# A hybrid decoder block on one core: norms and memory attention planned together with the causal attention, token tiles first

## The chip, the cores and the metric

The kernel runs on one core of one Trainium2 chip. The metric is the device time of one execution in microseconds; the time before is a median of 3 runs, 1797.26 us (1796.97 to 1797.59).

## The reference, cut to what matters

A decoder block over 1024 tokens of width 1024, with 256 memory tokens. Three gated branches run in parallel on the normed tokens, and a squared-ReLU MLP follows.

```python
h = rmsnorm(x, g_mix_norm)                         # x: 1024 x 1024
proj = h @ w_in                                    # sb q,k,v | fox q,k,v | forget | mem q | gates
o_sb  = stick_breaking_attention(sb_q, sb_k, sb_v)            # 8 heads of 64, causal
o_fox = forgetting_attention(norm(fx_q), norm(fx_k), fx_v, log_f)   # 8 heads of 64, causal
mh = rmsnorm(mem, g_mem_norm)                      # mem: 256 x 1024
mk, mv = split(mh @ w_mem_kv)                      # 4 heads of 128
o_mem = softmax(norm(mq) @ norm(mk).T / sqrt(128)) @ mv
x = x + (sum of gate_b * (o_b @ w_branch_b)) @ w_out
x = x + relu(rmsnorm(x) @ w_ff_up)**2 @ w_ff_down
```

Every product is taken in float32 accuracy by splitting each operand into a high part (a rounded copy, made on ScalarE) and a low part (the rest, made on VectorE), and by three matmuls: high by high, high by low, low by high.

## The kernel before, in words

**Names.** PE, DVE, ACT, POOL and SP are TensorE, VectorE, ScalarE, GpSimd and SyncE. `hTh` and `hTl` (tiles `hi`, `lo` in the trace) hold the normed tokens, transposed, high and low. `whi`, `wlo` are the split weights, `raw` the weights as loaded, `xt` a tile of 128 tokens by 1024, `st` a small tile of statistics with 1 to 16 columns, `gb` the norm's gain spread over 128 partitions, `xg` a tile times its gain, `xs` half a normed tile. Buffers of memory banks: `pp` for dense products, `sc` for scores, `tr` for transposes, `pv` for attention outputs.

**First part, written out by hand (lines 649 to 877).** The order of the code is the order of issue, which the compiler's tile scheduler may loosen a little. `normed_T` (L165) norms one tile: on ACT a square with a running sum (L163), on DVE the inverse root in 11 small steps (`rsqrt`, L124 to 137: a seed in two steps, and three rounds of three), a scaling, on PE eight 128x128 transposes (L186), on ACT the high part (L189) and on DVE the low part (L190). The two memory tiles are normed first, with the gain and the scaling in one DVE step (L181) that reads the spread gain from a bank. The eight token tiles follow, two ahead of each of the four memory key and value projections (`norm_x`, L678); their gain is multiplied in on POOL, as two halves of 128x512 (L172), and the scaling is a DVE step (L179). `halves` and `load_w` load and split the weights, `natural` takes the products (`mm3`, L157 to 159). Then come the queries of the memory attention (`mem_queries`), the memory attention itself (`mem_attention`, L753 to 791) and the first pair of stick-breaking heads' queries and keys.

**Second part, a planner (from L876).** At build time a small event simulation, the `Machine`, decides the order of the instructions. Processes are Python generators that yield an `Op` (an engine, an estimated cost, a function that emits instructions), `Get` a buffer, `Sleep`, or wait for an `Event`. An engine that is free in the simulation takes the ready operation with the lowest due time, and what it takes is emitted; each engine on the chip then runs its stream in that order. Attention units, dense projections (`Task`: gates, values, queries, keys), the weight loader and the first two branch products are such processes. Dense operations are marked `side`, and `PACE` says after how much dense work each attention unit may begin. A dense operation is a piece of at most 6 matmuls of 512 columns (`PIECE`) or 12 of 256. The forgetting attention scales its softmax rows on DVE (L1143).

**Third part (from 945 us on in the profile):** the third branch, the output projection and the MLP, ordered by hand.

## Time and profile before

| | before |
|---|---|
| median of 3 runs | 1797.26 us |
| the profiled execution, time | 1799.35 us |
| its span | 1797.6 us |
| PE busy | 1758.4 us (98%) |
| DVE busy | 1287.7 us (72%) |
| ACT busy | 801.7 us (45%) |
| POOL busy | 160.4 us (9%) |

The profiled execution lies 2.1 us above the median of the runs, and its span is 1.75 us shorter than its own time. A row of the timeline reads: start, duration, engine, line, operation, output<-inputs, partitions x elements, and in brackets how long the engine had been idle and what ended it. Matmuls are pipelined: the duration of one includes its latency, so the rate of a stream is read from the distance of two starts. A row of the windows reads: the stretch, its length, then busy time and count of instructions of PE, PEld (its weight loads), DVE, ACT and POOL, then the granted TensorE clock, the DMA share and GB/s.

### The profile page before, as it was taken

The numbers are of one execution on the slowest core, as the hardware profiler recorded it, in microseconds if no ns is written. First come the engines' busy times: TensorE is split into PE (matmuls) and PEld (weight loads), VectorE is DVE, ScalarE is ACT, GpSimd is POOL, SyncE is SP. The second block draws the span as 40 slices with busy tenths as digits, with TensorE's granted clock in tenths as the row PEclk, the third lists the DMA queues.
The fourth block names the chain that finished last, engine by engine and source line by source line (L and its number), as shares of the span: only waits on it lengthen the run. The fifth ranks groups of instructions, "written<-read, shape, count | busy, mean of one in ns | idle before, by whom it ended". The sixth has DMA issues, their size and how long they took to land.

```text
span 1797.6 us, 26005 instructions
## 1 busy us (share of the span) xinstructions
PE 1758.4 (98%) x9800; PEld 1517.0 (84%) x9800; DVE 1287.7 (72%) x2221; ACT 801.7 (45%) x1466; POOL 160.4 (9%) x283
## 2 busy tenths in 40 slices
PE   8899999999999999999999999899999999999999
PEld 6797998889888899899888899787888888788887
DVE  7986666656756577777998752587777775878786
ACT  5355545545555466556754332433323334333332
POOL 2200101111111100000000012011121120000000
PEclk9998999999999999999999999999999999999999
DMA  6211111231231311212344552224444464545433
GB/s 201 70 54 47 30 39 48 68 94 31 68 95 57 89 52 43 71 52 75 119 149 139 164 191 82 95 88 141 146 147 157 139 213 153 178 169 170 157 117 135
DMA packets 137441, 194.67 MB, mean 108 GB/s; under 512 B 9826, under 2 KB 81506, under 8 KB 137316
## 3 DMA queue, kind: packets, MB, share of 16 engines
q1 hardware_dynamic: 128836, 165.22, 28.9%
q0 software_dynamic: 8480, 27.79, 4.4%
q8 instruction: 77, 1.26, 0.3%
q14 instruction: 48, 0.39, 0.1%
HBM read 137.67 MB, written 55.31 MB: 107 GB/s over the span
## 4 chain that ended last, share of the span: by engine, by line
PE 86%; DVE 9%; ACT 2%; issue 2%; DMA 1%; SPq 0%; POOL 0%; ACTq 0%; DVEq 0%; POOLq 0%
PE pp L1326 33%; PE pp L231 9%; PE pp L619 5%; PE sc L231 5%; PE pv L1198 4%; PE tr L1178 4%; PE pp L159 3%; PE pp L157 3%; PE pp L158 3%; PE sc L619 3%; PE tr L619 3%; PE tr L231 2%; PE pv L619 2%; PE sc L157 2%; PE sc L158 1%
## 5 line engine op out<-in xcount | busy, mean ns | idle before, releaser
L1326 PE MATMUL pp<-hi,whi 128*128 128x512 f32 x480 | 192.8, 402 | 0.0
L1326 PE MATMUL pp<-lo,whi 128*128 128x512 f32 x480 | 189.1, 394 | 0.0
L1326 PE MATMUL pp<-hi,wlo 128*128 128x512 f32 x480 | 188.9, 394 | 0.0
L231 PE MATMUL pp<-h,oh 128*128 128x512 f32 x512 | 160.2, 394 | 2.7 <-ACT cu L398 2.7
L1326 PE MATMUL pp<-whi,hi 128*128 128x256 f32 (+1 forms) x512 | 145.6, 284 | 0.0
L1326 PE MATMUL pp<-whi,lo 128*128 128x256 f32 (+1 forms) x512 | 143.9, 281 | 0.0
L1326 PE MATMUL pp<-wlo,hi 128*128 128x256 f32 (+1 forms) x512 | 143.8, 281 | 0.0
L1185 DVE TENSOR_TENSOR ptl<-tr,pth 128x512 fp32r<-128x512 f32 (+1 forms) x160 | 100.0, 633 | 45.3 <-ACT pth L1183 44.5
L1183 ACT ACTIVATE pth<-tr 128x512 fp32r<-128x512 f32 (+1 forms) x160 | 87.1, 557 | 94.2 <-PE tr L1178 53.1
L619 PE MATMUL pp<-h,sop 128*128 128x512 f32 x504 | 118.6, 392 | 0.0
L231 PEld LDWEIGHTS pp<-h,oh 128*128 128x128 f32 x512 | 96.0, 188 | 25.0 <-ACT cu L398 3.5
L619 PEld LDWEIGHTS pp<-h,sop 128*128 128x128 f32 x504 | 94.5, 188 | 21.5 <-DVE sop L252 0.9
L1326 PEld LDWEIGHTS pp<-hi,wlo 128*128 128x128 f32 x480 | 90.2, 188 | 21.4
L1326 PEld LDWEIGHTS pp<-hi,whi 128*128 128x128 f32 x480 | 90.4, 188 | 16.2
L1326 PEld LDWEIGHTS pp<-lo,whi 128*128 128x128 f32 x480 | 90.5, 189 | 15.8
L231 PE MATMUL pp<-h,ol 128*128 128x512 f32 x256 | 101.0, 395 | 0.0
L1094 DVE TENSOR_TENSOR_SCAN r<-r,sm 128x896 f32<-128x896 f32 (+3 forms) x64 | 87.6, 1369 | 14.5 <-POOL r L1089 14.3
L1326 PEld LDWEIGHTS pp<-wlo,hi 128*128 128x128 f32 x512 | 96.5, 188 | 0.4
L1326 PEld LDWEIGHTS pp<-whi,hi 128*128 128x128 f32 x512 | 96.4, 188 | 0.4
L1326 PEld LDWEIGHTS pp<-whi,lo 128*128 128x128 f32 x512 | 96.5, 189 | 0.0
L1251 DVE TENSOR_TENSOR wlo<-raw,whi 128x1024 fp32r<-128x1024 f32 (+1 forms) x58 | 70.6, 1219 | 31.2 <-ACT whi L1250 30.7
L1198 PE MATMUL pv<-pth,v 128*128 128x256 f32 x320 | 85.4, 289 | 0.0
(373 smaller groups left out, 4590.3 us busy)
## 6 DMA issues: line engine op xcount, KB each, us to landing
raw<-w_in SPq DMA_DIRECT2D x42, 512.0 KB
raw<-w_up SPq DMA_DIRECT2D x64, 256.0 KB
s_scr<-s POOLq DMA_DIRECT2D x56, 256.0 KB, 2.7
ur<-s_scr SPq DMA_DIRECT2D x14, 1024.0 KB
gate_scr<-o SPq DMA_DIRECT2D x48, 256.0 KB
s_scr<-cu POOLq DMA_DIRECT2D x42, 256.0 KB, 2.9
ur<-s_scr SPq DMA_DIRECT2D x14, 768.0 KB
o<-gate_scr SPq DMA_DIRECT2D x32, 256.0 KB
```

Source lines behind the costliest of these rows:

```text
L157: nc.tensor.matmul(ps, lh, rh, start=(i == 0), stop=False)
L158: nc.tensor.matmul(ps, lh, rl, start=False, stop=False)
L159: nc.tensor.matmul(ps, ll, rh, start=False, stop=(i == n - 1))
L231: nc.tensor.matmul(ps, w[a_][:, k * P:(k + 1) * P], h[b_][k], start=(first and k == 0 and i == 0), stop=(last and k == 3 and i == 2), skip ...
L619: nc.tensor.matmul(ps, a_[:, c, q], b_[:, c, :], start=(kind in ("P1", "P2", "P7") and c == 0 and i == 0), stop=(kind in ("P2", "P4", "P3" ...
L1094: nc.vector.tensor_tensor_scan(out=rev, data0=rev, data1=zero.to_broadcast([P, n]), initial=1.0, op0=ALU.mult, op1=ALU.add)
L1178: nc.tensor.transpose(tr[:, jj * 256 + a * P:jj * 256 + (a + 1) * P], es[a][:, j * P:(j + 1) * P], ident)
L1183: yield Op("ACT", act_time(512 - lo_c), lambda: nc.scalar.activation(ph[:, lo_c:], tr[:, lo_c:], AF.Copy))
L1185: yield Op("DVE", dve_time(512 - lo_c), lambda: nc.vector.tensor_tensor(pl[:, lo_c:], tr[:, lo_c:], f32(ph[:, lo_c:]), ALU.subtract))
L1198: nc.tensor.matmul(pv[0][:, c_:256], v_of[key][:, j, h4, :], p_[:, jj * 256 + c_:(jj + 1) * 256], start=(k == 0 and n_ == 0 and i == 0), s ...
L1251: yield Op("DVE", dve_time(m), lambda: nc.vector.tensor_tensor(lo, raw, f32(hi), ALU.subtract))
L1326: nc.tensor.matmul(ps, a_, b_, start=(first and i == 0), stop=(last and i == n - 1))
```

## The change

1. The planner moves ahead of the first part, and the whole first part becomes its processes. `prologue` starts the token tiles in groups, [x0], [x1], [x2, x3], [x4, x5], [x6, x7], and then the memory tiles [m0, m1]; `norm` takes one inverse root per group, so there are six of 11 steps where there were ten. Every tile but the first gets its gain on POOL, in place and whole (128x1024), and one DVE scaling of 128x1024. `xt` has 7 buffers.
2. Both gains are spread to `gb` by four matmuls of one row at the very start (`spread`).
3. The first dense task is the values of the first stick-breaking heads, which need only token tiles and start as these come; the four memory projections (`dense_kv`), the first pair's queries and keys and the memory queries (`dense_mq`) follow as dense tasks, and the memory attention is a planned process whose scores and products mingle with dense work. The causal units wait for the memory keys, values and queries.
4. A dense operation is a piece of three matmuls of 512 columns, or six of 256.
5. The scaling of the forgetting attention's softmax goes from DVE to ACT. The copies of the memory keys and queries out of their banks go from DVE to ACT as well (`head_squares`).
6. The planner's model of a load becomes a shared pipe (250 bytes per ns and 2.0 us), `PACE` goes from 80 to 66 for the first four pairs, and `Machine.choose` lets an operation that needs another ACT table wait up to 4 us for others with the loaded one.

```diff
-    def load_time(size):
-        return 2.3 + size / 180e3
+    def transfer(fn, size, issue=0.1):
+        yield Op("SP", issue, fn, 0.0)
+        machine.pipe = max(machine.now, machine.pipe) + size / 250e3
+        yield Sleep(machine.pipe + 2.0 - machine.now)
...
+    N = Pool("n0", gb=2, xt=7, xj=1)
...
-    PIECE = mm_time(512) * 6
+    PIECE = mm_time(512) * 3
...
+    def norm(keys, late):
...
+        def gain(xt):
+            yield spread_
+            yield Op("POOL", 2.6, lambda: nc.gpsimd.tensor_tensor(xt, xt, gb, ALU.mult))
+        for i, key in enumerate(keys):
...
+            yield Op("ACT", 1.25, lambda: nc.scalar.activation(junk, xt, AF.Square, accum_out=ss[:, i:i + 1]))
+            if by_pool:
+                gained.append(spawn(gain(xt)))
+        r = yield from rsqrt_ops(ss, n, 1.0 / D)
+        for i, key in enumerate(keys):
+            xt, ri, s = x_in[key][0], r[:, i:i + 1], key[1]
+            if by_pool:
+                yield gained[i]
+                yield Op("DVE", 0.67, lambda: nc.vector.tensor_scalar(xt, xt, ri, None, ALU.mult))
...
+                evs.append(spawn(norm_half(key, xt, k4), late))
...
+        keys = [[("x", 0)], [("x", 1)], [("x", 2), ("x", 3)], [("x", 4), ("x", 5)], [("x", 6), ("x", 7)],
+                [("m", 0), ("m", 1)]]
+        spawn(fetch_tokens([k for ks_ in keys for k in ks_]))
+        evs = [spawn(norm(ks_, 3.0 * i), 3.0 * i) for i, ks_ in enumerate(keys)]
...
-            nc.vector.tensor_scalar(e[:, :n], e[:, :n], rl, None, ALU.mult)
...
+        yield Op("ACT", act_time(n), lambda: nc.scalar.activation(e[:, :n], e[:, :n], AF.Copy, scale=rl))
...
-                for k in range(0, KD, 2):
-                    ab = [x_ for kk in (k, k + 1) for x_ in passes(tuple(t[:, kk, :] for t in w),
-                                                                   (hTh[:, kk, cs], hTl[:, kk, cs]))]
+                for k in range(KD):
+                    ab = passes(tuple(t[:, k, :] for t in w), (hTh[:, k, cs], hTl[:, k, cs]))
...
+    h_tasks += [kv_tasks[0], sb_projection(0, True), kv_tasks[1], sb_projection(0, False), *kv_tasks[2:], dense_mq(0), dense_mq(1)]
...
-    PACE = [80.0 * min(c, 4) + 60.0 * max(c - 4, 0) for c in range(9)]
+    PACE = [66 * min(c, 4) + 60 * max(c - 4, 0) for c in range(9)]
```

The counts of matmuls are the same. The order changes from the start to the middle; the last 3854 PE instructions, from inside the second branch on, and the last 733 of DVE stand in the same order in both kernels.

POOL at the start of the program, in the order of issue. In the kernel before, each token tile `xt` gives two halves of a separate tile `xg`:

```order
L172 TENSOR_TENSOR xg_220<-xt_215,gb_191 128x512 x2
L172 TENSOR_TENSOR xg_265<-xt_260,gb_191 128x512 x2
L172 TENSOR_TENSOR xg_404<-xt_399,gb_191 128x512 x2
L172 TENSOR_TENSOR xg_449<-xt_444,gb_191 128x512 x2
L172 TENSOR_TENSOR xg_588<-xt_583,gb_191 128x512 x2
L172 TENSOR_TENSOR xg_633<-xt_628,gb_191 128x512 x2
L172 TENSOR_TENSOR xg_741<-xt_736,gb_191 128x512 x2
L172 TENSOR_TENSOR xg_786<-xt_781,gb_191 128x512 x2
```

POOL at the same place after the change. `xt_126` to `xt_131` are the token tiles x1 to x6, `xt_125` is x7, and the last two rows, with the gain `gb_141`, are the memory tiles m0 and m1:

```order
L869 TENSOR_TENSOR xt_126<-xt_126,gb_140 128x1024
L869 TENSOR_TENSOR xt_127<-xt_127,gb_140 128x1024
L869 TENSOR_TENSOR xt_128<-xt_128,gb_140 128x1024
L869 TENSOR_TENSOR xt_129<-xt_129,gb_140 128x1024
L869 TENSOR_TENSOR xt_130<-xt_130,gb_140 128x1024
L869 TENSOR_TENSOR xt_131<-xt_131,gb_140 128x1024
L869 TENSOR_TENSOR xt_125<-xt_125,gb_140 128x1024
L869 TENSOR_TENSOR xt_126<-xt_126,gb_141 128x1024
L869 TENSOR_TENSOR xt_127<-xt_127,gb_141 128x1024
```

Eight tiles in sixteen steps became nine tiles in nine steps, since the memory tiles now go this way too and only x0 does not.

DVE in the middle of the start-up, before: the end of an inverse root (L133 to 136) with the low part of a weight and of a memory tile in between, then the two scalings of the first token tile:

```order
L136 SCALAR_TENSOR_TENSOR st_235<-st_232,st_230 128x1
L133 SCALAR_TENSOR_TENSOR st_237<-st_235 128x1
L150 TENSOR_TENSOR wlo_390<-raw_387,whi_389 128x1024
L190 TENSOR_TENSOR v_99<-tr_184,v_99 128x4x128
L134 TENSOR_TENSOR st_237<-st_237,st_223 128x1
L136 SCALAR_TENSOR_TENSOR st_240<-st_237,st_235 128x1
L179 TENSOR_SCALAR xs_242<-xg_220,st_240 128x512
L179 TENSOR_SCALAR xs_244<-xg_220,st_240 128x512
```

DVE after, at the end of the start-up: the last rounds of the memory tiles' inverse root (L821 to 823, two columns at once), between them the scaling (L884) of x7 (`xt_125`) and then of m0 (`xt_126`), and the low parts (L915) of what PE has transposed:

```order
L821 SCALAR_TENSOR_TENSOR st_420<-st_421 128x2
L822 TENSOR_TENSOR st_420<-st_420,st_418 128x2
L823 SCALAR_TENSOR_TENSOR st_419<-st_420,st_421 128x2
L884 TENSOR_SCALAR xt_125<-xt_125,st_380 128x1024
L821 SCALAR_TENSOR_TENSOR st_420<-st_419 128x2
L822 TENSOR_TENSOR st_420<-st_420,st_418 128x2
L823 SCALAR_TENSOR_TENSOR st_421<-st_420,st_419 128x2
L884 TENSOR_SCALAR xt_126<-xt_126,st_421 128x1024
L915 TENSOR_TENSOR lo_98<-tr_109,hi_97 128x4x128
L915 TENSOR_TENSOR lo_98<-tr_110,hi_97 128x4x128
L1538 TENSOR_TENSOR v_123<-pp_106,v_123 128x8x64
```

The memory tiles, which opened DVE's work before, now close the start-up.

PE at its first rows, before: the spread of the memory gain, the transposes of the first memory tile, and the first products with it (`v_99` holds the normed memory):

```order
L200 MATMUL sc_107<-row_104 128x512
L200 MATMUL sc_109<-row_104 128x512
L186 MATMUL tr_137<-ident,xs_133 128x128 x4
L186 MATMUL tr_144<-ident,xs_135 128x128 x4
L157 MATMUL pp_307<-whi_205,v_99 128x256
L158 MATMUL pp_307<-wlo_206,v_99 128x256
L159 MATMUL pp_307<-whi_205,v_99 128x256
```

PE after, where the last normed tile (m1, `xt_127`) is transposed: ahead of it and behind it stand products with the values' weights (`whi`, `wlo`, L1466) and token tiles, and then the first products of 512 columns, with other weights (`whi_136`):

```order
L1466 MATMUL pp_104<-wlo_133,hi_97 128x256
L1466 MATMUL pp_104<-whi_132,lo_98 128x256
L906 MATMUL tr_109<-ident,xt_127 128x128 x4
L906 MATMUL tr_110<-ident,xt_127 128x128 x4
L1466 MATMUL pp_104<-whi_134,hi_97 128x256
L1466 MATMUL pp_104<-wlo_135,hi_97 128x256
L1466 MATMUL pp_104<-whi_134,lo_98 128x256
```

What PE does ahead of m1 is now only transposes and the values of the token tiles.

More of the change, by code (lines that the diff above doesn't have):

```diff
@@ new lines, in tile_hybrid_block, with spread @@
+    h_made, m_made = [Event() for _ in range(ST)], [Event() for _ in range(2)]
+    x_in, two_in = {}, Event()
+    gains = {k: (N.t("gb", [P, D]), Event()) for k in ("x", "m")}
+    junk = N.t("xj", [P, D])
+    ones_ = OB.free.popleft()
+    ones = ones_[:1, :P]
+    def spread(key, rows, landed):
+        gb, ev = gains[key]
+        yield landed
+        for half in range(2):
+            cs = slice(half * 512, half * 512 + 512)
+            sc = yield Get(SC)
+            yield Op("PE", 4 * mm_time(512), lambda: nc.tensor.matmul(
+                sc, ones, rows[half][:1], start=True, stop=True))
+            yield Op("ACT", act_time(512), lambda: nc.scalar.activation(gb[:, cs], sc, AF.Copy))
+            SC.put(sc)
+        machine.fire(ev)
@@ L1228, in units @@
     def units(large):
+        yield kv_over
+        for ev in mq_made.values():
+            yield ev
+        base = machine.side
         for c, pair in enumerate(pairs):
@@ L1445, in may @@
             n = 8 if keys else 4
-            if len(HT.free) < n:
+            if len(HT.free) < n or c and not all(ev.fired for ev in mq_made.values()) or not keys and sb_taken[0] < 2 * c + 1 \
+                    or keys and sb_taken[0] < 2 * c:
                 return False
+            sb_taken[0] += 1
             tiles_.extend(HT.free.popleft() for _ in range(n))
@@ L1800, in all_h @@
         machine.fire(closed)
[L1802 removed]
+    PACE = [66 * min(c, 4) + 60 * max(c - 4, 0) for c in range(9)]
     with tc.manual_schedule():
+        spawn(prologue())
+        for load in h_tasks[0].loads:
+            spawn(first_weights(load))
+        spawn(memory())
+        spawn(after_kv(kv_tasks))
         spawn(all_h([t.done for t in h_tasks]))
```

651 lines of the change are left out of this document (355 added, 296 removed).

## The prediction

> **What bounds the kernel now.** I first read the page's busy times and its slices, to see which engine is short and where.
>
> ```profile
> PE 1758.4 (98%) x9800; PEld 1517.0 (84%) x9800; DVE 1287.7 (72%) x2221; ACT 801.7 (45%) x1466; POOL 160.4 (9%) x283
> PE   8899999999999999999999999899999999999999
> DVE  7986666656756577777998752587777775878786
> PEclk9998999999999999999999999999999999999999
> ```
>
> PE is busy 98% of the span, and only three slices of 45 us fall below nine tenths: the first two and one near 900 us. In the second slice DVE stands at nine. Next I read the windows over the stretches that the change touches.
>
> ```profile
> core 0: us, PE busy (x) PEld busy (x) DVE busy (x) ACT busy (x) POOL busy (x), PEclk, DMA share, GB/s
> 0.00:45.00 45.00, 36.16 (x221) 30.69 (x222) 35.14 (x98) 24.48 (x36) 11.07 (x14) 0.96 0.65 201
> 45.00:90.00 45.00, 36.03 (x272) 34.06 (x271) 41.78 (x119) 16.29 (x28) 12.57 (x10) 0.92 0.24 69
> 90.00:135.00 45.00, 44.56 (x335) 41.79 (x334) 37.14 (x89) 23.27 (x59) 0.00 (x0) 1.00 0.18 54
> 135.00:180.00 45.00, 40.72 (x194) 32.67 (x193) 29.64 (x71) 24.23 (x61) 0.00 (x0) 0.89 0.15 47
> 180.00:800.00 620.00, 619.36 (x3864) 552.52 (x3862) 412.33 (x712) 327.56 (x667) 61.92 (x129) 1.00 0.21 59
> 800.00:945.00 145.00, 142.53 (x854) 124.74 (x854) 125.06 (x308) 91.84 (x195) 0.00 (x0) 0.99 0.37 114
> 945.00:1798.00 853.00, 839.07 (x4074) 700.48 (x4072) 606.64 (x827) 293.99 (x426) 74.80 (x130) 1.00 0.43 147
> ```
>
> From 180 to 800 us PE idles 0.64 us, and from 800 to 945 us 2.47 us. The rest of the program has one order in both kernels. So what can be won lies in the first 180 us. There PE idles 22.5 us by these rows, but the loss is larger, since a busy matmul at half clock hides some. I count the work instead, by the forms that PE runs there and the distance of two starts.
>
> ```profile
> L157 PE MATMUL pp<-whi,hi 128*128 128x256 f32 x128 | 37.0, 291 | 0.3 <-ACT hi L189 0.3
> L186 PE MATMUL tr<-ident,xs 128*128 128x128 f32 x80 | 12.8, 306 | 4.7 <-DVE xs L179 3.3 <-DVE xs L181 1.4
> L158 PE MATMUL pp<-lo,whi 128*128 128x512 f32 x32 | 12.8, 399 | 0.0
> L200 PE MATMUL sc<-row 1*128 1x512 f32 x8 | 6.1, 882 | 5.9 <-DVE st L129 5.9
> ```
> ```profile
> 17.54 0.28 PE L158 MATMUL pp<-wlo,v 128*128 128x256 f32 x1
> 17.66 0.28 PE L159 MATMUL pp<-whi,v 128*128 128x256 f32 x1
> ```
> ```profile
> 78.71 1.07 PE L186 MATMUL tr<-ident,xs 128*128 128x128 f32 x8 [0.20 <-DVE xs L179]
> ```
> ```profile
> 873.05 0.40 PE L1326 MATMUL pp<-lo,whi 128*128 128x512 f32 x1
> 873.28 0.39 PE L1326 MATMUL pp<-hi,wlo 128*128 128x512 f32 x1
> ```
>
> With all lines of a form together, the first 180 us hold 681 matmuls of 256 columns, 140 of 512, and 184 transposes. Warm, one of 256 starts 0.12 us after the last, one of 512 0.23 us; eight transposes take 1.07 us with about 0.28 us of latency at the end, so 0.11 us each. The work is 681 x 0.12 + 140 x 0.23 + 184 x 0.11 + 6.1 for the spread gains = 140.2 us. **PE loses 39.8 us of the first 180.** This is the pot.
>
> **The change, part by part.**
>
> *The start-up.* After the change PE's order up to m1's transposes holds 180 products of 256 columns, 72 transposes and the spread: 180 x 0.12 + 72 x 0.11 + 6.1 = 35.6 us. If PE gets past m1 at the time T, it has lost T - 35.6 by then. T is set by DVE, which norms every tile; I add up DVE's rows in the new order up to m1's scaling.
>
> ```profile
> 0.81 0.86 SPq L666 DMA_DIRECT2D xt<-mem  x2
> 1.72 0.33 SPq L196 DMA_DIRECT2D row<-g_memn  x1
> ```
> ```profile
> 4.33 1.06 ACT L163 ACTIVATE xg<-xt 128x1024 f32<-128x1024 f32 x1 [2.23 <-DMA xt<-mem]
> 5.29 0.19 ACT L163 ACTIVATION_READ_ACCUMULATOR xg<-xt 128x1 f32 x1
> ```
> ```profile
> 5.89 0.16 DVE L133 SCALAR_TENSOR_TENSOR st<-st 128x1 f32<-128x1 f32 x1
> 6.09 0.16 DVE L134 TENSOR_TENSOR st<-st,st 128x1 f32<-128x1 f32 x1
> ```
> ```profile
> L150 DVE TENSOR_TENSOR wlo<-raw,whi 128x1024 fp32r<-128x1024 f32 x14 | 18.2, 1300 | 1.5 <-ACT whi L149 1.3
> L190 DVE TENSOR_TENSOR lo<-tr,hi 128x512 fp32r<-128x512 f32 x16 | 10.4, 683 | 0.3 <-ACT hi L189 0.2
> L181 DVE SCALAR_TENSOR_TENSOR xs<-xt,st,sc 128x512 f32<-128x512 f32 x4 | 2.9, 746 | 0.0
> ```
> ```profile
> L1143 DVE TENSOR_SCALAR e<-e,st 128x1024 f32<-128x1024 f32 x8 | 6.0, 754 | 0.3
> ```
>
> The first tile's square began 3.5 us after its load was issued (0.81 to 4.33). In the changed kernel four rows of gains are issued ahead, 4 x 0.35 us by the row's 0.33, so x0 is there at about 5.7 us, and after 1.2 us of square and sum DVE begins at 6.9. Then it runs six inverse roots of 11 steps, 66 x 0.195 us (the distance of 5.89 and 6.09) = 12.9 us; three low parts of weights at 1.22 (unblocked; the row's mean of 1.30 holds waits) = 3.7; 18 low parts of tiles and three of values at 0.68 = 14.3; two scalings of x0 at 0.75 = 1.5; and nine scalings of 128x1024 at 0.754 = 6.8. Sum 39.2 us; with 3 us for the first transposes of x0, which nothing covers, DVE would scale m1 at 6.9 + 39.2 + 3 = 49 us.
>
> Against that stand the POOL gains. In this trace DVE hardly moves while POOL multiplies a gain:
>
> ```profile
> 47.13 2.54 POOL L172 TENSOR_TENSOR xg<-xt,gb 128x512 f32<-128x512 f32 x2 [9.85 <-DVE st L127]
> ```
> ```profile
> 47.33 1.09 DVE L133 SCALAR_TENSOR_TENSOR st<-st 128x1 f32<-128x1 f32 x1
> 48.46 1.22 DVE L134 TENSOR_TENSOR st<-st,st 128x1 f32<-128x1 f32 x1
> 49.72 0.16 DVE L136 SCALAR_TENSOR_TENSOR st<-st,st 128x1 f32<-128x1 f32 x1
> ```
>
> Two steps of 0.16 us took 2.31 us between them: 2.0 us lost to one tile's gain. The change has nine such gains, all inside the stretch that DVE bounds: 9 x 2.0 = 18 us. Its cost lies between 0 (every gain falls on a wait of DVE or on its steps that read a bank) and 9 x 2.4 = 21.6. I take 18, the row's own value, since DVE is nearly always occupied there. **T = 49 + 18 = 67 us.** The loss at m1 is 67 - 35.6 = 31.4 us. Ahead of that PE stands idle between tiles; what the slow clock costs after m1 is bounded by the row below.
>
> ```profile
> 13.18 0.41 PE L158 MATMUL pp<-wlo,v 128*128 128x256 f32 x1
> 13.39 0.41 PE L159 MATMUL pp<-whi,v 128*128 128x256 f32 x1
> ```
>
> From 12.8 to 17.4 us PE ran at 0.21 us a matmul instead of 0.12; 4.4 us of that costs 1.9. Behind m1 all tokens are normed, the next weights are loaded ahead, and products of 512 columns give PE a store of work which the kernel before hasn't got: there, 135:180 idles 4.28 us around the memory attention, 90:135 0.44. I take 2.8 for all of this stage, between the two. Sum: 31.4 + 1.9 + 2.8 = 36.1, against 39.8: **3.7 us gained.** The grouped roots save 44 steps x 0.195 = 8.6 us of DVE, the overlap of memory attention with dense work saves most of the 4.28; the waits of one more whole gain, and products that now wait for single tiles, give nearly all back.
>
> *The middle, 180 to 945.* 64 scalings of fox rows leave DVE (eight each of widths 128 to 1024; the widest 6.0 us in the row above) and come to ACT, with nine more table loads:
>
> ```profile
> L163 ACT ACT_TABLE_LOAD x1 | 1.3, 1283 | 0.8 <-PEq L1971 0.8
> ```
>
> 9 x 1.28 = 11.5 us, and some 35 us of scalings. ACT's cover is its idle time, 292 us of 620 and 53 of 145; without it each load holds a row of softmax by 1.3 us. Finer pieces on PE cost nothing that the trace shows (0.64 us idle in 620 with both kinds mixed), and `PACE` 66 only moves units. DVE is freed where it is shortest, 800 to 945 (125.06 of 145). At most 3.1 us is to be had (0.64 + 2.47); at worst the stage idles twice as long with ACT at nine tenths, 3 us lost. I take 0.5 gained.
>
> *Sum.* 3.7 + 0.5 = 4.2 us against the profiled execution's 1799.35, so 1795.15; that execution lies 2.1 above the median, so 1797.26 - 4.2 = **1793**.
>
> **What a rule makes of the gains.** The Trainium skill, "SBUF — State Buffer", section "SBUF: two separate sides", calls the port pair that DVE and GpSimd share an exclusive lock, held for a whole instruction. The two rows of 1.09 and 1.22 agree: one step slipped through between the two halves of the gain. By that rule the whole gain of 128x1024 lets nothing through in its middle; it is the second rival below.
>
> **The rivals.**
> 1. *The waits for POOL are small.* Gains may run ahead while DVE waits or works from banks; each tile's gain needs only the spread row and the tile, not the root. For it: 21 of the DVE steps read banks. Against: the rows at 47 us. Without the 18 us T is 49: gain 22.2, time 1775; half of them 1784.
> 2. *Whole gains block wholly.* A gain in one piece stops one step for its whole 2.54 us instead of letting one through at half: 9 x 2.4 = 21.6, 3.6 us more, time 1796.7.
> 3. *Slower: the clock.* PE gets a tile's 3.5 us of work about each 6 us, so its clock may stay at half, and the products then pile up behind the last tiles. For it: the clock fell with PE never idle when transposes and spread rows stood between products.
>
> ```profile
> 20.00:25.00 5.00, 5.00 (x24) 4.10 (x24) 4.76 (x9) 2.58 (x4) 2.88 (x2) 0.66 0.36 122
> ```
>
>    If the last 100 products (12 us warm) run at 0.21 behind m1's time, this adds 9.0 us: 1802. It turns slower by over 0.2% from 87 such products (7.8 us). Against it: each wait gives PE time to catch up. The Trainium skill, "TensorE: Matmul & The Clock Gate", section "Why this matters for your kernels", lets the clock fall only after an idle gap of some 3 us; by that the gaps here (6 - 3.5) would leave it at full and 1793 would stand. The row with 0.66 and no gap disagrees with it.
> 4. *The change doesn't do what it says:* pieces of three and the planned memory attention only reorder what PE never waited for (0.44 us in 90:135). Then the start-up alone decides, and the sum is that of the forecast.
>
> **How the numbers follow.** Forecast (with 4) 1789 to 1796: 0.40, of it 0.25 below 1793.7. Rival 1, 1772 to 1788: 0.24. Rival 2, 1795 to 1799: 0.16. Rival 3, 1801 to 1806: 0.20. A measurement of this kernel tells about 0.2%, 3.6 us, from no change. Faster by more: 0.25 + 0.24 = 0.49; within: 0.15 + 0.16 = 0.31; slower: 0.20. The range leaves out a quarter of rival 1 at the bottom and a sixth of rival 3 at the top: 1776 to 1804.
>
> **What would show it.** In the changed kernel m1's scaling (L884) should lie near 67 us, and PE's work up to 180 us should fall some 36 us short. Rival 1 shows m1 near 50 us and DVE steps of 0.16 us while L869 runs; rival 2 shows single small steps of 2.4 us; rival 3 shows PEclk well below 0.9 between 40 and 80 us with PE busy. If PE idles long behind m1, waiting for weights or for the memory's keys, the forecast is wrong at the 2.8 us; if 800 to 945 idles over 5 us, ACT's cover failed.

## The result, and the profile after

The changed kernel takes 1799.78 us (median of 20 runs, 1795.61 to 1801.18), the kernel before 1797.22 us (20 runs, 1795.91 to 1798.57): a ratio of 1.0011, 95% interval 1.0004 to 1.0018. It is slower by 0.11%, which is within the 0.2% taken for no change; forecast was 1793, 0.24% faster. The profiled execution took 1797.69 us, 2.1 us under the median, and the kernel before's lies 2.1 us above its own, so the two profiles show 1.7 us gained where the medians show 2.6 us lost; how executions of the changed kernel differ is told at the end.

First the page of the changed kernel: busy times and slices.

```profile
PE 1754.3 (98%) x9800; PEld 1515.6 (84%) x9800; DVE 1249.7 (70%) x2093; ACT 865.4 (48%) x1551; POOL 163.5 (9%) x276
PE   6999999999999999999999999899999999999999
DVE  7544667676776567667887752587777775878786
```

The first slice of PE is worse than before (six tenths, not eight), the second better (nine, not eight), and DVE has room from the second slice on, where it stood at nine. The windows over the stretches of the prediction:

```profile
core 0: us, PE busy (x) PEld busy (x) DVE busy (x) ACT busy (x) POOL busy (x), PEclk, DMA share, GB/s
0.00:45.00 45.00, 28.39 (x120) 21.31 (x120) 35.65 (x68) 21.77 (x37) 20.68 (x16) 0.92 0.53 176
45.00:90.00 45.00, 42.57 (x287) 38.61 (x288) 26.19 (x60) 18.45 (x29) 2.39 (x1) 1.00 0.17 48
90.00:135.00 45.00, 44.40 (x263) 38.78 (x263) 22.18 (x36) 17.22 (x25) 0.00 (x0) 1.00 0.38 108
135.00:180.00 45.00, 45.00 (x316) 41.78 (x315) 20.24 (x51) 18.83 (x38) 0.00 (x0) 1.00 0.20 57
180.00:800.00 620.00, 619.60 (x3896) 553.57 (x3895) 426.34 (x763) 382.05 (x773) 65.61 (x129) 1.00 0.21 61
800.00:945.00 145.00, 139.28 (x879) 123.63 (x878) 115.50 (x297) 108.57 (x218) 0.00 (x0) 0.99 0.33 104
```

The start pays after its first 45 us: there PE idles 16.6 us, where it idled 8.8, but then 2.4, 0.6 and 0 us per window, where it idled 9.0, 0.4 and 4.3, and the clock of 0.92 and 0.89 in two of these windows is at 1.00. The stretch from 800 to 945 us gives it back: 5.7 us idle against 2.5, although DVE is less busy there (115.5 against 125.1). ACT took its work over (108.6 against 91.8).

To compare kernels whose streams are in another order, I count PE's loss by its own position. Each matmul or transpose counts its warm distance to the next start (0.118 us for 256 columns, 0.231 for 512, 0.109 for a transpose and for 128, in proportion for other widths, and 0.53 for the one-row matmuls that spread a gain); the sum up to an instruction is its position, and what the starts lie further apart is loss. Sums of one profiled execution each, in us; "handover" is the part in which the last forgetting rows run beside the first branch products:

| | median time | start, 0 to 140 | 140 to 740 | handover, 740 to 970 | rest |
|---|---|---|---|---|---|
| before | 1797.22 | 43.0 | 2.6 | 6.2 | 11.8 |
| changed | 1799.78 | 31.9 | 2.7 | 15.9 | 11.5 |

So in these two executions 11.1 us come from the start, and 9.7 are lost at the handover: the spans differ by 1.7 us (1797.6 and 1795.9).

**The start.** POOL and DVE of the changed kernel where the gains of x2 and x3 run:

```profile
16.70 5.03 POOL L869 TENSOR_TENSOR xt<-xt,gb 128x1024 f32<-128x1024 f32 x2 [4.42 <-ACT xj L876]
```
```profile
17.15 2.30 DVE L821 SCALAR_TENSOR_TENSOR st<-st 128x1 f32<-128x1 f32 x1
19.49 2.26 DVE L822 TENSOR_TENSOR st<-st,st 128x1 f32<-128x1 f32 x1
21.79 0.16 DVE L823 SCALAR_TENSOR_TENSOR st<-st,st 128x1 f32<-128x1 f32 x1
```

Each of these two gains holds one step of 0.16 us for nearly its whole length. Over the nine gains seven small steps and two scalings are held, and the waits in them sum to 16.9 us. The scalings of the tiles in one row (their shortest, middle and longest duration in ns, then the first and the last start in us):

```profile
L884 DVE TENSOR_SCALAR xt<-xt,st x9: 742/750/2785, 22.1 to 62.2; 128x1024 f32<-128x1024 f32 x9
```

The scaling of m1 starts at 62.2 us; the prediction had 67.

**The handover.** The windows of the changed kernel from 815 us on, and what PE waited for from 800 to 1000 us (us in total, times, longest):

```profile
815.00:845.00 30.00, 27.76 (x183) 24.55 (x182) 21.73 (x51) 23.21 (x43) 0.00 (x0) 1.00 0.36 107
845.00:875.00 30.00, 30.00 (x212) 27.58 (x211) 25.17 (x69) 24.81 (x51) 0.00 (x0) 1.00 0.21 70
875.00:895.00 20.00, 16.52 (x88) 14.00 (x88) 19.30 (x54) 15.47 (x35) 0.00 (x0) 0.91 0.45 139
895.00:940.00 45.00, 45.00 (x254) 38.61 (x253) 37.10 (x95) 33.95 (x71) 0.00 (x0) 1.00 0.38 120
940.00:960.00 20.00, 17.42 (x90) 15.01 (x89) 15.34 (x37) 13.46 (x30) 0.00 (x0) 0.83 0.40 126
```
```profile
PE tr L1311 <- DVE ptl L1318: 2.8, 2, 1.9
PE tr L1311 <- ACT e L1283: 2.0, 2, 1.6
PE pv L1331 <- DVE ptl L1318: 1.1, 1, 1.1
PE pp L1466 <- DVE wlo L1388: 0.9, 1, 0.9
```

There are few waits, none over 2 us, and they come from several engines. In two of these windows the clock falls as well (0.91 and 0.83). The kernel before, over the same 800 to 1000 us, and its window at 940:

```profile
PE tr L1178 <- DVE h L1567: 2.2, 1, 2.2
PE tr L1178 <- DVE e L1143: 0.3, 1, 0.3
```
```profile
940.00:960.00 20.00, 20.00 (x115) 17.22 (x114) 18.25 (x46) 9.41 (x24) 0.00 (x0) 1.00 0.44 141
```

It waits 2.5 us in all, where the changed kernel waits 8.3 (three smaller lines included), and near 890 us its clock falls too (0.91 over 875 to 895). PE's timeline in the changed kernel at 948 us:

```profile
947.99 0.28 PE L1253 MATMUL sc<-h,h 68*128 68x256 f32 x1
949.92 0.98 PE L1311 MATMUL tr<-ident,e 128*128 128x128 f32 x7 [1.65 <-ACT e L1283]
951.83 1.11 PE L1311 MATMUL tr<-ident,e 128*128 128x128 f32 x4 [0.93 <-DVE ptl L1318]
952.59 0.56 PE L1331 MATMUL pv<-pth,v 128*128 128x256 f32 x1
952.95 0.41 PE L1331 MATMUL pv<-ptl,v 128*128 128x256 f32 x1
953.17 0.31 PE L1331 MATMUL pv<-pth,v 128*128 128x128 f32 x1
```

Two gaps, 1.65 and 0.93 us, with seven transposes between them, and then the products start 0.22 us apart instead of 0.12.

### The profile page after: what moved, and what is told of

Same layout as the page of the kernel before. It is cut to its first block, busy times and chain, and to the rows that moved or that the text cites. A ratio compares the mean times of both kernels' runs of the same rounds, so it can differ in the third digit from the quotient of the medians.

```text
span 1795.9 us, 25923 instructions
## 1 busy us (share of the span) xinstructions
PE 1754.3 (98%) x9800; PEld 1515.6 (84%) x9800; DVE 1249.7 (70%) x2093; ACT 865.4 (48%) x1551; POOL 163.5 (9%) x276
## 4 chain that ended last, share of the span: by engine, by line
PE 86%; DVE 9%; ACT 3%; issue 2%; DMA 0%; POOL 0%; SPq 0%; ACTq 0%; DVEq 0%; POOLq 0%
PE pp L1466 36%; PE pp L188 9%; PE pp L576 5%; PE sc L188 5%; PE pv L1331 4%; PE tr L1311 3%; PE sc L576 3%; PE tr L576 3%; PE tr L188 2%; PE pp L158 2%; PE pp L157 2%; PE pp L159 2%; PE pv L576 2%; PE sc L158 1%; PE sc L157 1%
## 5 line engine op out<-in xcount | busy, mean ns | idle before, releaser
L1466 PE MATMUL pp<-hi,whi 128*128 128x512 f32 x512 | 205.3, 401 | 0.0
L1466 PE MATMUL pp<-hi,wlo 128*128 128x512 f32 x512 | 202.2, 395 | 0.6 <-DVE wlo L1388 0.6
L1466 PE MATMUL pp<-lo,whi 128*128 128x512 f32 x512 | 201.4, 393 | 0.0
L1466 PE MATMUL pp<-whi,hi 128*128 128x256 f32 (+1 forms) x640 | 185.0, 289 | 0.6 <-ACT whi L1387 0.6
L1466 PE MATMUL pp<-wlo,hi 128*128 128x256 f32 (+1 forms) x640 | 182.2, 285 | 1.1 <-DVE wlo L1388 1.1
L1466 PE MATMUL pp<-whi,lo 128*128 128x256 f32 (+1 forms) x640 | 181.3, 283 | 0.0
L1466 PEld LDWEIGHTS pp<-wlo,hi 128*128 128x128 f32 x640 | 122.5, 191 | 2.6 <-DVE wlo L1388 1.6
L1388 DVE TENSOR_TENSOR wlo<-raw,whi 128x1024 fp32r<-128x1024 f32 (+1 forms) x72 | 87.7, 1221 | 52.8 <-ACT whi L1387 52.6
L1466 PEld LDWEIGHTS pp<-whi,hi 128*128 128x128 f32 x640 | 122.4, 191 | 1.7 <-ACT whi L1387 0.8
L1466 PEld LDWEIGHTS pp<-whi,lo 128*128 128x128 f32 x640 | 122.6, 192 | 0.3 <-DVE lo L915 0.3
L1466 PEld LDWEIGHTS pp<-hi,wlo 128*128 128x128 f32 x512 | 96.2, 188 | 23.8 <-DVE wlo L1388 1.0
L1466 PEld LDWEIGHTS pp<-lo,whi 128*128 128x128 f32 x512 | 96.4, 188 | 17.1
L1466 PEld LDWEIGHTS pp<-hi,whi 128*128 128x128 f32 x512 | 96.4, 188 | 16.6
L1227 DVE TENSOR_TENSOR_SCAN r<-r,sm 128x896 f32<-128x896 f32 (+4 forms) x64 | 87.6, 1371 | 17.5 <-POOL r L1222 17.2
```

The source lines that it names most:

```text
L1227: nc.vector.tensor_tensor_scan(out=rev, data0=rev, data1=zero.to_broadcast([P, n]), initial=1.0, op0=ALU.mult, op1=ALU.add)
L1388: yield Op("DVE", dve_time(m), lambda: nc.vector.tensor_tensor(lo, raw, f32(hi), ALU.subtract))
L1466: nc.tensor.matmul(ps, a_, b_, start=(first and i == 0), stop=(last and i == n - 1))
```

## The experiments

All times are medians; a ratio is to the kernel before, with its 95% interval. Where a kernel keeps the plan's order, only the engine that runs one operation is changed, in its old place of the order. The handover's 9.7 us had at first two explanations: the softmax scaling now waits in ACT's queue (theory 1), or the attention, begun 57 us later (its first product of values at 266 us against 209), ends too late against the dense work (theory 2). Three more came with later runs: the planner's new model of a load plans weights earlier than they come (theory 3), the small pieces leave attention work without a margin (theory 4), or the loss is a few single waits, with half clock behind them, that any new plan draws anew (theory 5).

**The scaling back on DVE** (`fox_dve`), order kept.

```diff
-        yield Op("ACT", act_time(n), lambda: nc.scalar.activation(e[:, :n], e[:, :n], AF.Copy, scale=rl))
+        yield Op("ACT", act_time(n), lambda: nc.vector.tensor_scalar(e[:, :n], e[:, :n], rl, None, ALU.mult))
```

> The changed kernel with the forgetting attention's softmax scaling emitted on DVE again, in the place where the plan has it on ACT, so that the order on every other engine stays as it is. Theory 1 (the scaling waits in ACT's queue behind copies of the branches' operands, and PE's transposes wait for it between 820 and 960 us): the wait of 1.65 us at 949 us and the half clock behind it go, 4 to 6 us of the 9 that the handover loses come back, about 1795 us. Theory 2 (the attention starts 57 us later than before and ends in the same place, so it is packed too tightly, whichever engine scales): no change within 1.5 us, or slower, since DVE gets some 15 us more between 815 and 960 us: 1800 to 1803 us.

Measured: 1800.83 us, 1.0027 (1.0016 to 1.0038). No better than the changed kernel. The handover lost 20.6 us in its profile (which is of its longest run, 1806.81 us). Theory 1 falls as an account of the 9.7 us.

**The scaling on ACT alone** (`before_fox_act`), order kept.

```diff
-            nc.vector.tensor_scalar(e[:, :n], e[:, :n], rl, None, ALU.mult)
+            nc.scalar.activation(e[:, :n], e[:, :n], AF.Copy, scale=rl)
```

> The kernel before with that one scaling put on ACT, in its place in the order; nothing else of the change. Theory 1: the handover gets worse, 3 to 6 us, 1800 to 1803 us. Theory 2: within 1.5 us of 1797, or 1 to 2 us faster, because DVE is the fuller engine there (13.3 of 15 us at 880 to 895).

Measured: 1800.03 us, 1.0017 (1.0008 to 1.0025). Slower by 3.1 us, but not at the handover (6.1 us there, as before); 2.4 us more lie at positions 140 to 740, where PE now waits 1.9 us for these rows and waited 0.5. So the move is no gain by itself, and its price is elsewhere than theory 1 had it.

**The gain on DVE** (`gain_dve`): the norm's gain goes into the DVE scaling, POOL multiplies no gain in the start; order kept.

```diff
-            yield Op("POOL", 2.6, lambda: nc.gpsimd.tensor_tensor(xt, xt, gb, ALU.mult))
+            yield Op("POOL", 2.6, lambda: None)
...
-                yield Op("DVE", 0.67, lambda: nc.vector.tensor_scalar(xt, xt, ri, None, ALU.mult))
+                yield Op("DVE", 0.67, lambda: nc.vector.scalar_tensor_tensor(xt, xt, ri, gb, ALU.mult, ALU.mult))
```

> The changed kernel with the norm's gain taken into the DVE scaling of each tile (one step of 128x1024 with two inputs in memory) instead of POOL; order otherwise kept. If the waits for POOL's gains cost DVE 16.9 us as its long small steps add up to, and each scaling grows from 0.75 to about 1.3 us (9 x 0.55 = 5), the scaling of m1 moves from 62 to about 50 us and the loss of the first 180 us falls from 31.6 to about 21: 8 to 11 us faster than the changed kernel, 1789 to 1792. If the handover only moves with the start (its places are set by the order of PE's stream, so it keeps its loss), all of that shows in the time. Rival: PE's order and half clock bound the start, not DVE; then under 3 us.

Measured: **1783.38 us**, 0.9929 (0.9917 to 0.9942), 16.4 us under the changed kernel, more than expected. Its scalings, and its first windows:

```profile
L884 DVE SCALAR_TENSOR_TENSOR xt<-xt,st,gb x9: 1275/1279/1286, 16.6 to 48.7; 128x1024 f32<-128x1024 f32 x9
```
```profile
0.00:45.00 45.00, 37.18 (x212) 29.92 (x213) 34.96 (x101) 27.10 (x46) 1.09 (x8) 1.00 0.52 176
45.00:90.00 45.00, 44.45 (x276) 39.14 (x275) 23.79 (x43) 20.21 (x29) 0.00 (x0) 1.00 0.26 73
```

DVE does more work, 9 x 0.53 = 4.8 us, and yet m1 is scaled 13.5 us earlier: 18.3 us of waits went with POOL's gains. PE has 9 us more of busy time in the first 45. The start's loss falls from 31.9 to 18.4 us, the handover's stays (14.7). Of the new start's loss of 31.9 us, 13.5 are thus shown to be the waits for POOL, net of the longer scalings.

**Gains in halves** (`gain_halves`), order kept.

```diff
-            yield Op("POOL", 2.6, lambda: nc.gpsimd.tensor_tensor(xt, xt, gb, ALU.mult))
+            yield Op("POOL", 2.6, lambda: [nc.gpsimd.tensor_tensor(xt[:, c_:c_ + 512], xt[:, c_:c_ + 512], gb[:, c_:c_ + 512], ALU.mult)
+                                           for c_ in (0, 512)])
```

> The changed kernel with each POOL gain in two instructions of 128x512 instead of one of 128x1024, nothing else. If a gain holds DVE's steps for the whole instruction, halves let one more small step of 0.16 us through per gain: DVE steps of at most 1.2 us instead of 2.3, a little less waiting, 0 to 2 us faster than the changed kernel (1798 to 1800). If it isn't the instruction that is held, the long steps stay at 2.3 us and the time is the same.

Measured: 1799.75 us, 1.0009 (1.0000 to 1.0018): no difference. DVE's rows where the gains of x4 and x5 run:

```profile
28.21 1.24 DVE L815 TENSOR_SCALAR st<-st 128x2 f32<-128x2 f32 x1
29.49 1.21 DVE L816 TENSOR_SCALAR st<-st 128x2 int32<-128x2 int32 x1
30.73 1.18 DVE L821 SCALAR_TENSOR_TENSOR st<-st 128x2 f32<-128x2 f32 x1
```

The long steps are half as long and there are twice as many. What holds DVE is the instruction on POOL, one step each; the total is POOL's time.

**A pace of 60, 63, 57 and 69** (`pace60` and the others): one number, and the plan is made anew.

```diff
-    PACE = [66 * min(c, 4) + 60 * max(c - 4, 0) for c in range(9)]
+    PACE = [60 * min(c, 4) + 60 * max(c - 4, 0) for c in range(9)]
```

> The changed kernel with the four stick-breaking pairs paced by 60 us of dense work each instead of 66, so that every attention unit is planned earlier against the dense work, by up to 24 us at the last four pairs. Theory 2 (the attention, begun 57 us later, ends too late, and the last forgetting rows find too little dense work beside them and the branches' operands come late): PE's loss between 810 and 1035 us, 20.3 us in the changed kernel against 10.9 before, falls by a third or more, 3 to 8 us faster, 1792 to 1797. If it isn't where the attention ends, the units only crowd more earlier on: the same loss, 1799 to 1802.

> The changed kernel with the first four pairs paced by 63 us of dense work, half way between the 66 of the changed kernel and the 60 that took PE's loss at the handover (by PE's own position, 740 to 970 us of its work) from 15.9 to 7.1 us. Theory 2 (the attention ends too late against the dense work): the loss goes down steadily with the pace, so about 11 to 12 us here and a time of about 1794 to 1796. Theory 5 (the loss is made by a few single waits of 2 us, each with half clock behind it, and any new plan draws them anew): no order in it; anything from 6 to 20 us, 1789 to 1803.

> The changed kernel paced by 57 us, one step beyond 60. Theory 2: the loss at the handover stays at or under 7 us, and the time at or under 1789 us, until the attention is so early that its units crowd (then the loss moves ahead of position 740). Theory 5: no order; it may as well come back to 1795 to 1803.

> The changed kernel paced by 69 us, one step the other way. Theory 2: the loss at the handover grows beyond 15.9 us, by 3 to 6 us, and the time to 1802 to 1807. Theory 5: no order, 1789 to 1805.

Measured, with the dense work that PE has done at the attention's last product (by position, as above):

| pace | time | ratio | handover loss | dense work done at the last product |
|---|---|---|---|---|
| 57 | 1788.83 | 0.9960 (0.9948 to 0.9973) | 7.8 | 654 |
| 60 | 1789.53 | 0.9964 (0.9951 to 0.9976) | 7.1 | 654 |
| 63 | 1795.41 | 0.9990 (0.9981 to 0.9999) | 6.1 | 666 |
| 66 (changed) | 1799.78 | 1.0011 (1.0004 to 1.0018) | 15.9 | 672 |
| 69 | 1794.78 | 0.9995 (0.9986 to 1.0004) | 12.4 | 682 |

At 60 the two windows that had a slow clock in the changed kernel read:

```profile
875.00:895.00 20.00, 18.73 (x101) 14.97 (x101) 17.35 (x41) 16.89 (x36) 0.00 (x0) 1.00 0.45 149
940.00:960.00 20.00, 20.00 (x111) 17.10 (x110) 15.87 (x37) 12.19 (x25) 0.00 (x0) 1.00 0.39 117
```

The slow clock is gone from both, and the idle time at 940 to 960 too. With 66 and 69 PE waits there, with 57, 60 and 63 it doesn't: that much is theory 2. But the loss steps rather than grows: 63 lost 6.1 us where theory 2 had 11 to 12, and 69 lost less than 66 where it had more. 63 also lost more elsewhere (35.7 at the start, 6.4 in the middle). So part of theory 5 stands as well.

**The same pace in the kernel before** (`before_pace84`): 84 instead of 80, nothing of the change.

```diff
-    PACE = [80.0 * min(c, 4) + 60.0 * max(c - 4, 0) for c in range(9)]
+    PACE = [84.0 * min(c, 4) + 60.0 * max(c - 4, 0) for c in range(9)]
```

> The kernel before with the first four pairs paced by 84 us of dense work instead of 80; nothing of the change. The last four pairs then stand 16 us later against the dense work, with the three-quarter point of the attention's products at about 591 us of it instead of 575, as in the changed kernel (594). Theory 2: the loss at the handover grows from 6.2 to 12 to 16 us, the time to 1803 to 1807. Theory 5: no order; most likely within 3 us of 1797.

Measured: 1800.62 us, 1.0022 (1.0013 to 1.0031); the handover loses 11.3 us instead of 6.2, and the last product stands at 671 us of dense work instead of 664. (The three-quarter point that I had named did not move, 575 in both; it was the wrong mark, the last product is the better one.) PE's longest waits there:

```profile
PE tr L1541 <- DVE r L1585: 3.3, 1, 3.3
PE tr L1178 <- DVE ptl L1185: 2.4, 2, 1.6
```

So a later attention goes with a larger loss in a kernel without any other part of the change as well, though 11.3 us and 1800.62 are less than theory 2 had (12 to 16, and 1803 to 1807). A pace makes a new plan each time, so lateness is not separated here from whatever else the plan moves.

**The old model of a load** (`old_load`), a new plan.

```diff
-        machine.pipe = max(machine.now, machine.pipe) + size / 250e3
-        yield Sleep(machine.pipe + 2.0 - machine.now)
+        yield Sleep(2.3 + size / 180e3)
```

> The changed kernel with the planner's old model of a load (2.3 us and 180 bytes per ns, no shared pipe) in place of the new one; the plan is otherwise made by the same rules. Theory 3 (the new model lets weights be planned earlier than they come, PE's waits for whi and wlo at 828 and 830 us, 1.4 us and what follows from them): the loss between 810 and 1035 us falls by 2 to 6 us, 1794 to 1798. Otherwise: the same within 2 us.

Measured: 1791.47 us, 0.9968 (0.9956 to 0.9980); the handover loses 7.3 us, though its last product stands at 673. PE's waits for weights at 828 us are gone, and the 1.65 us at 949; two waits of 0.3 and 0.9 us stand near there instead, and the clock stays at 1.00. The time falls by 8.3 us, more than the 2 to 6 of theory 3. Late is therefore not always dear; this run speaks for theories 3 and 5, and doesn't tell them apart.

**KEEP at 0** (`keep0`).

```diff
-    KEEP = 4.0
+    KEEP = 0.0
```

> The changed kernel with KEEP at 0, so that ACT always takes the operation that is due first, whatever table it needs, as the kernel before does. More table loads than the 17 of the changed kernel are then in ACT's stream, at 1.28 us each. If ACT's order under KEEP makes the softmax rows late in the handover (an operation may wait up to 4 us in the plan), the loss between 810 and 1035 us falls, 2 to 5 us faster; if KEEP saves loads that would stand in the path, it is 2 to 10 us slower.

Measured: 1798.65 us, 1.0010 (1.0001 to 1.0018), with 17 table loads as in the changed kernel. The rule saves none here; neither expectation had anything to act on.

**Pieces.** The old pieces in the changed kernel (`piece6`; three loops, the first shown), then with a pace of 60 (`piece6_pace60`), then with the softmax scaling emitted on DVE (`piece6_fox_dve`), and the new pieces alone in the kernel before (`before_piece3`).

```diff
-    PIECE = mm_time(512) * 3
+    PIECE = mm_time(512) * 6
...
-                for k in range(KD):
-                    ab = passes(tuple(t[:, k, :] for t in w), (hTh[:, k, cs], hTl[:, k, cs]))
-                    last = yield Op("PE", PIECE, products(ps, ab, k == 0, k == KD - 1), side=True, goes_on=True)
+                for k in range(0, KD, 2):
+                    ab = [x_ for kk in (k, k + 1) for x_ in passes(tuple(t[:, kk, :] for t in w),
+                                                                   (hTh[:, kk, cs], hTl[:, kk, cs]))]
+                    last = yield Op("PE", PIECE, products(ps, ab, k == 0, k == KD - 2), side=True, goes_on=True)
```

> The changed kernel with the dense products in the old pieces of six matmuls of 512 columns, or twelve of 256. Theory 4 (three-matmul pieces let the planner set attention work on PE into places where the chip's operands aren't there yet, since it has no margin any more): the loss between 810 and 1035 us falls to 11 to 15 us and the time to 1792 to 1796. If pieces only give PE more places to fill a wait, coarser ones cost 1 to 5 us: 1801 to 1805.

> The changed kernel with the old, larger pieces and the pace of 60. With larger pieces alone the handover lost 30.5 us, with the pace of 60 alone 7.1. If the pieces act by a mechanism of their own (attention work waits on PE behind a piece, and the next one waits for it), 18 to 25 us are lost here, 1800 to 1808. If the lateness of the attention is all, 7 to 10: 1789 to 1793.

> The changed kernel with the old, larger pieces, and the softmax scaling emitted on DVE in its place of the plan. In piece6 PE waits 7.1 us for ACT's exponentials and 4.6 us for its scalings between 800 and 1000 us. If ACT's queue, longer by the scalings, is what makes large pieces dear, 10 us or more of the 30.5 come back: 1805 to 1810. If it is the order of PE (score steps with no dense piece between them), the waits remain: 1815 to 1822.

> The kernel before with the dense products of its planned part in pieces of three matmuls (six of 256 columns), nothing else of the change. If small pieces are worth something by themselves, the 6.2 us at the handover fall to 2 to 4 and the time to 1793 to 1795. If they only mend what the rest of the change makes worse: within 2 us of 1797. A new plan may also draw a single wait more or less: plus or minus 3 us.

Measured: 1817.24 us (1.0111, 1.0097 to 1.0125), 1819.45 (1.0122, 1.0109 to 1.0136), 1822.35 (1.0138, 1.0124 to 1.0152), with 30.5, 34.8 and 34.5 us lost at the handover; `before_piece3` 1796.60 (0.9993, 0.9984 to 1.0002), with 6.3. What PE waited for between 800 and 1000 us in `piece6`, and its largest single wait:

```profile
PE sc L1252 <- ACT e L1270: 7.1, 2, 5.1
PE tr L1311 <- ACT e L1283: 4.6, 3, 2.0
PE tr L1668 <- DVE r L1715: 4.0, 1, 4.0
```
```profile
832.03 0.49 PE L1252 MATMUL sc<-h,h 128*128 128x512 f32 x1
832.36 0.40 PE L1253 MATMUL sc<-h,h 68*128 68x512 f32 x1
837.87 0.58 PE L1252 MATMUL sc<-h,h 128*128 128x256 f32 x1 [5.12 <-ACT e L1270]
```

Score steps follow each other with no dense piece between them, and the next waits until ACT's exponentials are through. Taking the scalings off ACT does not help, nor does the pace, and all three lose more than any expectation had; theory 4, by which larger pieces would have helped, falls. That leaves the order on PE as the likely cause, but no run changed that order alone. Small pieces are worth 17.5 us in the changed kernel and nothing that the measurement shows in the kernel before. Which of the plan's other rules makes large pieces dear here was not found.

**The gain on DVE in the kernel before** (`before_gain_dve`).

```diff
-            normed_T(xt, gbx, hTh, hTl, s * P, N, ss, True)
+            normed_T(xt, gbx, hTh, hTl, s * P, N, ss)
```

> The kernel before with the gain of the token tiles taken into their DVE scaling (two steps of 128x512 with two inputs in memory at 0.75 us instead of 0.48) and not multiplied in on POOL. The waits of DVE for POOL go, 8 gains x 2.0 = 16 us, and 16 x 0.27 = 4.3 us come in addition. If DVE's waits bound that start too: 6 to 12 us faster, 1785 to 1791. If that start is bound by its chain of memory projections and weights, with POOL's gains beside: under 3 us.

Measured: 1791.65 us, 0.9973 (0.9963 to 0.9983), 5.3 us faster; the start's loss goes from 43.0 to 37.1. Less than the 6 to 12 expected where DVE's waits bound the old start: they seem to be only partly in PE's way.

**Both stages mended** (`gain_dve_pace60`: gain on DVE and pace 60; `best_old_load`: with the old model of a load as well).

> The changed kernel with the gain in the DVE scaling (16.4 us faster alone, start loss 31.9 to 18.4) and the pace of 60 (10.3 us faster alone, handover loss 15.9 to 7.1). If start and handover are separate stages, whose losses are set by the order of each, the two add up: about 1799.8 - 16.4 - 10.3 = 1773 us. If the loss of the handover depends on when PE arrives there, the sum falls short, 1776 to 1783.

> The changed kernel with the gain in the DVE scaling, the pace of 60 and the old model of a load. If pace and load model work on one loss, which the pace has taken already (7.4 us are left at the handover), nothing is added: 1774 to 1779. If they work on two, some 5 us more: 1770 to 1773.

Measured: 1776.80 us, 0.9885 (0.9870 to 0.9901), and **1774.73 us, 0.9876 (0.9863 to 0.9890)**, the best version found, 22 us under the kernel before. The first falls 3.7 us short of the sum of its two parts (1773). The handover loses nearly the same whether PE arrives earlier or later (7.4 us, and 7.1 with the pace alone); the start loses 20.2 us, and 18.4 with the gain alone. Where the rest of the 3.7 us comes from was not found. The second lost 20.1 at the start and 3.5 at the handover; of the 5 us that two separate losses would have given, 2 came.

## Why the prediction was wrong

By its own steps:

- **The pot.** It had 39.8 us lost in the first 180; by the finer distances 43.0. Right in kind: the start is where the change won. One line was misread: the third slice below nine tenths is the 26th, from 1123 us on, not near 900; it lies in the third part and plays no role.
- **T, when DVE scales m1.** 67 us predicted, 62.2 measured. The waits for POOL were sized rightly: 18 us predicted, 16.9 in the long steps of the trace, 18.3 by `gain_dve`. That its m1 lies at 48.7 us, beside the 49 of the sum without waits, is chance: it holds 4.2 us of longer scalings ahead of m1, so the sum was 4.5 too high. The rest of the 5 us came from adding durations where two starts lie closer (low parts 0.60 us apart, not 0.68; scalings 0.66, not 0.75; 3.2 us of overlap up to m1) and from counting m1's own scaling ahead of its start (0.75). The 3 us of uncovered waiting were about right: the gaps over 0.3 us behind the first tile sum to 2.6. The start then lost 31.9 us where 36.1 were forecast, and with the larger pot it gained 11.1 us in the profiled execution, not 3.7. The memory attention, whose products now stand between 177 and 254 us among dense work, left PE next to no idle time (0.40 us from 180 to 800).
- **The middle.** This is the step that failed: "I take 0.5 gained", with at worst 3 us lost. Measured: 9.7 us lost at the handover. I had looked at which engine was full there, found DVE, and reckoned that taking work off DVE helps. The engine's load was not the limit: `fox_dve` gives DVE its work back, and the time stays. What moved the loss is where the plan puts the units: `PACE` 66 sets the last attention products at 672 us of dense work instead of 664, and waits appear at 940 to 960 us. Pace alone moved this loss in both kernels (15.9 to 7.1; 6.2 to 11.3), so the sentence "`PACE` 66 only moves units" was the error. Over all runs, the piece runs of the changed kernel left out, six plans with that last product at 666 or less lose 3.5 to 7.8 us at the handover; of five at 671 or more four lose 11.3 to 15.9 (20.6 in the longest run of `fox_dve`), and `old_load` 7.3. Why a late end makes these waits is argued, not shown.
- **ACT's scalings.** No gain at all, and alone 3.1 us slower; they took ACT 49.7 us, not some 35. The cover of ACT's idle time was an average and no cover for a row that PE waits for next, as the longer waits in `before_fox_act` suggest. The prediction's sign that this cover failed, more than 5 us idle from 800 to 945, came (5.7), but `fox_dve` shows that ACT was not the reason.
- **Pieces.** "Cost nothing that the trace shows" was right for the kernel before (0.9993) and missed that the new plan depends on them (17.5 us).

Of the rivals, the second had the right mechanism (a whole gain holds a step for its whole length) with a total no larger than halves have. The first gave 1775 us for a kernel without waits for POOL; `gain_dve_pace60` took 1776.80, but with longer scalings and the handover mended, so the closeness is chance. The third, the clock, is there in some executions, as told below. The range's upper end leaves out two fifths of this rival's span, not a sixth. The measured time lies in the range by luck: a start that was underrated by 7.4 us and a middle that was overrated by 10.2 nearly cancel in the profiles.

Not settled: why `old_load` loses little though it ends late, and what makes single waits in the handover.

## What to carry to other kernels

An engine that is not the bound can hold the one that is: before giving GpSimd a share of elementwise work, compare the time that it saves VectorE with the time in which VectorE stands still (here 4.8 us saved, 18 lost). When a planner's start is changed, count for its end as well: work that begins 57 us later may have to be paced so that it ends no later, and the place to look is the dense work that is left beside its last unit. A change of 11 us gained and 10 lost reads as no change; a table of PE's loss by its own position takes the two apart.

## What the runs showed of the hardware

- In this start a GpSimd gain with two inputs in memory (128x1024 in 2.35 us) holds VectorE's steps from memory to memory; a step of 0.16 us takes up to 2.33. Only steps of 0.15 us that begin together with a gain get through (one at 10.08 us in the gain from 9.94 on). The Trainium skill, "SBUF — State Buffer", section "SBUF: two separate sides", states a lock held for the whole instruction; `gain_halves`, with steps of 1.2 us and no gain in time, agrees. Low parts, which read a bank, pass. In the changed kernel the second of these two low parts ran inside m1's gain at its usual length, and the step of 0.16 us behind it waited:

```profile
46.64 2.39 POOL L869 TENSOR_TENSOR xt<-xt,gb 128x1024 f32<-128x1024 f32 x1 [1.68 <-ACT xj L876]
```
```profile
46.01 1.28 DVE L915 TENSOR_TENSOR lo<-tr,hi 128x512 fp32r<-128x512 f32 x2
47.21 1.83 DVE L821 SCALAR_TENSOR_TENSOR st<-st 128x2 f32<-128x2 f32 x1
```

- The start-up has two outcomes under one order. In `fox_dve`, whose order on PE is that of the changed kernel, the last gain began 1 us earlier (45.66 us, not 46.64), held a DVE step of 0.16 us ahead of a low part, and PE waited 5.0 us for that low part instead of 1.9:

```profile
45.76 2.26 DVE L822 TENSOR_TENSOR st<-st,st 128x2 f32<-128x2 f32 x1
48.13 1.28 DVE L915 TENSOR_TENSOR lo<-tr,hi 128x512 fp32r<-128x512 f32 x2
```
```profile
48.87 1.12 PE L906 MATMUL tr<-ident,xt 128*128 128x128 f32 x4 [5.01 <-DVE lo L915]
```
```profile
50.00:60.00 10.00, 10.00 (x69) 10.00 (x69) 6.93 (x24) 2.78 (x5) 0.00 (x0) 0.77 0.00 1
```

  The clock then stayed low until about 54 us (0.77 of full over 50 to 60 us, with PE never idle), and the start lost 35.6 us instead of 31.9. `keep0` and `pace63` show the same (35.5, 35.7); `gain_halves`, `pace57`, `pace60` and `pace69` are with the changed kernel (31.4 to 31.7). The 3.7 us are two thirds of what the changed kernel's runs spread (5.6 us, against 2.7 of the kernel before); that they make the spread was not measured run by run.
- The clock fell to half after gaps of 1.65 and 0.93 us with transposes between (948 to 953 us in the changed kernel, shown above), without any single long one. If transposes count for nothing, the gap there is 4.5 us, which this place alone can't exclude. In `fox_dve` one gap of 2.11 us was enough, with products running until 892.7 us; behind it they start 0.22 us apart:

```profile
894.80 0.58 PE L1331 MATMUL pv<-ptl,v 128*128 128x256 f32 x1 [2.11 <-DVE ptl L1318]
895.17 0.42 PE L1331 MATMUL pv<-pth,v 128*128 128x256 f32 x1
895.39 0.41 PE L1331 MATMUL pv<-ptl,v 128*128 128x256 f32 x1
```

  The gap of some 3 us that "TensorE: Matmul & The Clock Gate" of the Trainium skill (section "Why this matters for your kernels") asks for was not needed; what the measurement shows decides.
